# The same program with its SBUF tiles at other addresses: a hybrid decoder layer on one core

## The chip, the core and the metric

The kernel runs on one core of a Trainium2 chip. The metric is the device time of one execution in microseconds (us). The five engines of the core are called PE (TensorE: matrix products; its weight loads are shown apart as PEld), DVE (VectorE), ACT (ScalarE), POOL (GpSimd) and SP (SyncE, which issues DMA transfers). SBUF is the on-chip memory: 128 partitions, in each of which a tile occupies the same byte range. "Address" below means the byte offset in a partition. PSUM is the memory that matrix products are written to.

## What is computed

One decoder layer for 256 tokens of width 2048, in float32. The reference, cut to what matters here:

```python
h = layer_norm(x, ln_in_g, ln_in_b)
parts = split(h @ w_in)                        # LRU group, NSA attention group, memory-attention queries
o_lru = rg_lru_group(...)                      # causal conv, gated linear recurrence, times gelu gate
o_nsa = nsa_group(...)                         # compressed, selected and window attention, 8 heads of 64
o_mem = memory_group(mem_q, mem, w_mem_kv)     # 4 heads of 128 into 256 memory tokens
h = layer_norm(alpha * h + concat(o_lru, o_nsa, o_mem) @ w_out, ln1_g, ln1_b)
up = causal_dwconv(h @ w_up)                   # 2048 -> 2 x 5632
h = layer_norm(alpha * h + (gelu(up_g) * up_u) @ w_down, ln2_g, ln2_b)
```

## The kernel before, in words

All weights are streamed from HBM in chunks of 128 partitions x 1024 float32 (512 KB), in one fixed list of steps (`chunk`, line 93). `run` (171) takes the steps in order; `advance` (143) keeps loads, splits and products apart by a few steps. Every chunk is loaded by SP into one of 4 buffers `raw` (107), rounded by ACT to fp32r into one of 4 buffers `wH` (127), and the rest, raw minus wH, is written by DVE into one of 3 buffers `wL` (135). Activations are held in the same two parts. A product is then three PE products, summed in PSUM: high x high, high x low and low x high.

PE has two operands. The stationary one is a block of 128 x 128 that is loaded into the array (LDWEIGHTS, PEld in the trace); the moving one is streamed through it (MATMUL). Two helpers issue nearly all of them:

- `t_mm` (190, products on lines 194, 195, 197): the weights are stationary and the transposed activations `h` move, 256 columns at a time. 24 products a chunk. It serves the projection w_in (28 column blocks, about 60 to 290 us of the run) and the up projection (88 column blocks, about 390 to 886 us).
- `m_mm` (200, lines 205, 206, 208): the activations are stationary and the weights move, 512 columns at a time. It serves the output projection w_out (activations `oH`, `oL`; about 300 to 390 us), the down projection (`actH`, `actL`; about 886 to 1135 us), half of the memory projection, and the chunks `wvg` with 280 columns.

The first 60 us are the memory projection; its other half is on line 272, where `oH`, `oL`, which hold the split memory tokens there, move by 256 columns past `wH`, `wL`.

In the last column group of w_out, some chunks are split into tiles that are free by then instead of `wH` and `wL`: `lruR`, `lruI`, `lruT`, `qmem`, `kmem`, `vmem`, `qn`, `xc0` (the argument `alt`, 842). In the last column group of the down projection the eight tiles `h0` to `h7` serve so (922).

Tiles get their addresses from pools, in the order in which a pool's tiles are first asked for: first `fix` (60), which lives throughout, then `ws` (61) with raw, wH and wL, then `sm` (62), and last `mx` (65), the tiles of the mixers, whose place is given to the pool `ff` (966) with `actH`, `actL` and four gain and bias tiles after the output projection. Every tile named so far that holds 1024 float32 is 4096 bytes long, so buffers of one name lie at the same place modulo 4096. The order of the work does not depend on the addresses: the schedule is written by hand (66).

Of the kernel before, what the change touches and what calls it, by code (L numbers as in the profile page):

```python
# [21 lines left out]
F32 = mybir.dt.float32  # L22
F32R = mybir.dt.float32r
BF = mybir.dt.bfloat16
# [6 lines left out]
S = 256  # L31
KT = D // 128
# [23 lines left out]
def hymba_layer(ctx, tc, x, memT, params, rows, wab, w1, wmem, win, wvg, wout, wup, wdn, out):  # L56
# [3 lines left out]
    fix = ctx.enter_context(tc.tile_pool(name="fix", bufs=1))  # L60
# [4 lines left out]
    mx = mixstack.enter_context(tc.tile_pool(name="mx", bufs=1))  # L65
    ctx.enter_context(tc.manual_schedule())

    prm = fix.tile([128, NP1], F32, name="prm")
    prm2 = mx.tile([128, NP - NP1], F32, name="prm2")
    hq = [fix.tile([128, 4, S], F32R, name="h%d" % i) for i in range(8)]  # L70

    def hH(kt, cols=slice(0, S)):
# [2 lines left out]
    def hL(kt, cols=slice(0, S)):  # L75
        return hq[4 + kt // 4][:, kt % 4, cols]
    res = fix.tile([128, 2, D], F32, name="res")
    negh = fix.tile([128, 1], F32, name="negh")
    identb = fix.tile([128, 128], BF, name="identb")
    diagb = fix.tile([128, 2, 128], BF, name="diagb")  # L80
    cmaskb = fix.tile([128, 2, 60], BF, name="cmaskb")
    ident = prm[:, _P["ident"]]

    def P(name, i=0, n=1):
# [134 lines left out]
        V.tensor_scalar(dst, src, mv[:, 0:1], rs[:, 1:2], op0=OP.subtract, op1=OP.mult)  # L219


    oH = mx.tile([128, KT, S], F32R, name="oH")
    oL = mx.tile([128, KT, S], F32R, name="oL")
    mraw = {}

    def aH(kt, cols):
# [232 lines left out]
                  done_vg if kts[-1] == KT - 1 else None)  # L459


    kcmp = mx.tile([128, 32], F32, name="kcmp")
    vcmp = mx.tile([128, 2, 64], F32, name="vcmp")
    hidv = mx.tile([64, 2, 4, 32], F32, name="hidv")
    hidk = mx.tile([64, 32], F32, name="hidk")

    def cmp_mm(a):
        def mm(w, _):
# [92 lines left out]
            split_act(oH[:, 12 + h, :], oL[:, 12 + h, :], o[:, :S])  # L561
            yield

    cv = mx.tile([128, 2, 8], F32, name="cv")

    def lru_consts():

        t = mx.tile([128, 6, 8], F32, name="lc")
        lam = P("lam", 0, 8)
        ab, e, z, z2, s, den = (t[:, i, :] for i in range(6))  # L570
        V.tensor_scalar(z, lam, -1.0, None, op0=OP.mult)
        V.tensor_tensor(ab, z, lam, op=OP.max)
        A.activation(e, ab, AF.Exp, scale=-1.0)
        V.tensor_scalar(den, e, 2.0, None, op0=OP.add)
        V.reciprocal(den, den)
        yield
        V.tensor_scalar(ab, z, 0.0, None, op0=OP.max)
        V.tensor_mul(z, e, den)
        V.tensor_mul(z2, z, z)
        V.tensor_scalar(s, z2, 1.0 / 17, 1.0 / 15, op0=OP.mult, op1=OP.add)  # L580
        for k in (13, 11, 9, 7, 5, 3, 1):
            V.tensor_mul(s, s, z2)
            V.tensor_scalar(s, s, 1.0 / k, None, op0=OP.add)
            if k % 4 == 3:
                yield
        V.tensor_mul(s, s, z)
        V.scalar_tensor_tensor(s, s, 2.0, ab, op0=OP.mult, op1=OP.add)
        V.tensor_scalar(cv[:, 0, :], s, -8.0, None, op0=OP.mult)
        V.tensor_scalar(cv[:, 1, :], s, 8.0, None, op0=OP.mult)
        yield  # L590
# [35 lines left out]
            yield  # L626

    pcd = mx.tile([128, 4, 128], F32, name="pcd")
    pc = mx.tile([128, 128], F32, name="pc")
    outs = {}  # L630

    def nsa_gates(q, g):
# [73 lines left out]
        yield  # L706


    st1 = [fix.tile([128, 24], F32, name="st%d" % i) for i in range(2)]
    KORD = [12, 13, 14, 15, 8, 9, 10, 11, 0, 1, 2, 3, 4, 5, 6, 7]  # L710

    def residual(acc, m, nb, st):
# [358 lines left out]
```

## Time and profile before

| | |
|---|---|
| median of 3 runs | 1147.9 us (1147.19 to 1149.84) |
| the profiled execution, its own time | 1146.88 us |
| its span, first to last instruction | 1145.1 us |
| PE busy | 1120.7 us (98%) |
| PE weight loads busy (beside PE) | 1029.3 us (90%) |
| DVE busy | 734.6 us (64%) |
| ACT busy | 565.3 us (49%) |
| DMA, mean over the span | 185 GB/s |

Busy time is the union of an engine's instructions. Products on PE overlap: one is shown as 279 ns long where the next one starts after some 117 ns, so the rate is read from start times and not from the mean of one. A group line gives the line of the kernel, engine, operation, what it writes and reads, shapes, the count, busy time and the mean of one, and behind the last bar the idle time before it.

### The profile page before, as it was taken

Reading aid. Unit: us, or ns where it says so; the run is one execution under the profiler, and the core shown is the slowest. Engines: PE = TensorE matmul, PEld = TensorE weight load, DVE = VectorE, ACT = ScalarE, POOL = GpSimd, SP = SyncE. Lnnn points to the kernel's source line nnn. Section 1 sums busy time; section 2 is a strip of 40 time slices with the busy share of each in tenths; the row PEclk is TensorE's granted clock in tenths of the full one; section 3 lists DMA queues with packets and bytes.
Section 4 is the critical chain, followed back from the end, with each engine's and each line's share of the span. In section 5 each row is a group of like instructions: output and inputs, shape, how many; then the busy total and the mean of one; then the engine's idle time right before and its main releaser. Section 6 shows DMA issues by size and latency. Waiting matters only on the chain. (4 is left out here: it accounts for less than half of the span.)

```text
span 1145.1 us, 19315 instructions
## 1 busy us (share of the span) xinstructions
PE 1120.7 (98%) x7848; PEld 1029.3 (90%) x7848; DVE 734.6 (64%) x1073; ACT 565.3 (49%) x829; POOL 15.3 (1%) x26
## 2 busy tenths in 40 slices
PE   8999999999999899999999999999999999999996
PEld 7889878899988799999999999999999888888884
DVE  6778645567856776666666666666666845454546
ACT  5744444567744555555555555555555433343440
POOL 0200000000000000000000000000000000000000
PEclk9999999999999999999999999999999999999998
DMA  9666322344566466556565656555555776666662
GB/s 339 236 230 218 112 92 93 110 148 151 175 196 181 144 244 197 184 185 188 181 200 176 201 183 198 184 185 186 182 199 179 227 244 197 189 191 193 188 197 93
DMA packets 58984, 211.81 MB, mean 185 GB/s; under 512 B 6544, under 2 KB 6672, under 8 KB 58768
## 3 DMA queue, kind: packets, MB, share of 16 engines
q1 hardware_dynamic: 57024, 203.25, 54.9%
q0 software_dynamic: 1872, 7.34, 1.9%
q8 instruction: 61, 1.00, 0.4%
q14 instruction: 27, 0.22, 0.1%
HBM read 208.47 MB, written 2.10 MB: 184 GB/s over the span
## 5 line engine op out<-in xcount | busy, mean ns | idle before, releaser
L135 DVE TENSOR_TENSOR wL<-raw,wH 128x1024 fp32r<-128x1024 f32 (+2 forms) x367 | 441.5, 1215 | 163.0 <-PE sc L208 118.4
L127 ACT ACTIVATE wH<-raw 128x1024 fp32r<-128x1024 f32 (+2 forms) x367 | 375.6, 1046 | 200.2 <-PE sc L206 163.7
L194 PE MATMUL acc<-h,wH 128*128 128x256 f32 x1152 | 281.1, 284 | 1.4 <-ACT h L187 1.4
L195 PE MATMUL acc<-h,wH 128*128 128x256 f32 x1152 | 276.1, 279 | 0.7 <-DVE h L188 0.7
L194 PEld LDWEIGHTS acc<-h,wH 128*128 128x128 f32 x1152 | 216.7, 188 | 2.1 <-ACT h L187 1.6
L195 PEld LDWEIGHTS acc<-h,wH 128*128 128x128 f32 x1152 | 217.3, 189 | 1.4 <-DVE h L188 1.1
L194 PE MATMUL sc<-h,wH 128*128 128x256 f32 x704 | 168.5, 280 | 0.0
L195 PE MATMUL sc<-h,wH 128*128 128x256 f32 x704 | 168.3, 279 | 0.0
L197 PE MATMUL acc<-h,wL 128*128 128x256 f32 x1152 | 158.8, 279 | 0.0
L197 PEld LDWEIGHTS acc<-h,wL 128*128 128x128 f32 x1152 | 145.3, 188 | 0.0
L195 PEld LDWEIGHTS sc<-h,wH 128*128 128x128 f32 x704 | 132.7, 188 | 0.0
L194 PEld LDWEIGHTS sc<-h,wH 128*128 128x128 f32 x704 | 131.8, 187 | 0.0
L197 PE MATMUL sc<-h,wL 128*128 128x256 f32 x704 | 97.4, 279 | 0.0
L877 DVE SCALAR_TENSOR_TENSOR tn<-sc,prm,tn 128x255 f32<-128x255 f32 x88 | 42.4, 482 | 82.6 <-ACT tn L874 81.0
L197 PEld LDWEIGHTS sc<-h,wL 128*128 128x128 f32 x704 | 89.0, 188 | 0.0
L877 DVE SCALAR_TENSOR_TENSOR tn<-acc,prm,tn 128x255 f32<-128x255 f32 x88 | 42.4, 482 | 44.1 <-ACT tn L874 42.5
L205 PE MATMUL sc<-wH,actH 128*128 128x512 f32 x168 | 66.0, 393 | 0.0
L205 PE MATMUL acc<-wH,actH 128*128 128x512 f32 x168 | 66.0, 393 | 0.0
L206 PE MATMUL acc<-wH,actL 128*128 128x512 f32 x168 | 65.7, 391 | 0.0
L206 PE MATMUL sc<-wH,actL 128*128 128x512 f32 x168 | 65.7, 391 | 0.0
L874 ACT ACTIVATE tn<-sc,prm 128x256 f32<-128x256 f32 x44 | 24.8, 564 | 63.4 <-PE sc L197 63.4
L208 PE MATMUL sc<-wL,actH 128*128 128x512 f32 x168 | 51.9, 390 | 0.0
(294 smaller groups left out, 1213.1 us busy)
## 6 DMA issues: line engine op xcount, KB each, us to landing
raw<-in_wup_dram SPq DMA_DIRECT2D x176, 512.0 KB, 4.3
raw<-in_wdn_dram SPq DMA_DIRECT2D x88, 512.0 KB, 4.3
raw<-in_win_dram SPq DMA_DIRECT2D x56, 512.0 KB, 3.3
raw<-in_wout_dram SPq DMA_DIRECT2D x32, 512.0 KB, 4.2
raw<-in_wmem_dram SPq DMA_DIRECT2D x15, 512.0 KB, 6.9
raw<-in_wvg_dram SPq DMA_DIRECT2D x5, 420.0 KB, 4.1
res<-in_x_dram SPq DMA_DIRECT2D x4, 512.0 KB, 7.6
g<-in_rows_dram POOLq DMA_DIRECT2D x4, 512.0 KB, 6.2
```

What stands on the lines that cost most here:

```text
L127: A.activation(h[:, s], raws[j][:, s], AF.Copy)
L135: V.tensor_sub(l[:, s], r[:, s], splits[j][0][:, s].bitcast(F32))
L194: T.matmul(acc, w, hH(kt), start=(first and a == 0), stop=False, skip_group_check=True)
L195: T.matmul(acc, w, hL(kt), start=False, stop=False, skip_group_check=True)
L197: T.matmul(acc, l[:, a * 128:(a + 1) * 128], hH(kt), start=False, stop=(last and a == n - 1), skip_group_check=True)
L205: T.matmul(acc, xh(kt, ms), h[:, w], start=(first and a == 0), stop=False)
L206: T.matmul(acc, xl(kt, ms), h[:, w], start=False, stop=False)
L208: T.matmul(acc, xh(kt, ms), l[:, a * N:(a + 1) * N], start=False, stop=(last and a == n - 1))
L874: A.activation(t, src, AF.Identity, scale=P("fcw", cb * 3 + 2), bias=P("fcb", cb))
L877: V.scalar_tensor_tensor(t[:, s:], src[:, :S - s], P("fcw", cb * 3 + k), t[:, s:], op0=OP.mult, op1=OP.add)
```

## The change

Tiles are asked for in another order, and a tile of 544 bytes that nobody uses is put in (`gap0`). No instruction is added, removed or moved, on any engine, and no wait: the two programs differ in addresses alone. The whole of it:

```diff
     prm = fix.tile([128, NP1], F32, name="prm")
+    kcmp = mx.tile([128, 32], F32, name="kcmp")
+    vcmp = mx.tile([128, 2, 64], F32, name="vcmp")
+    hidv = mx.tile([64, 2, 4, 32], F32, name="hidv")
+    hidk = mx.tile([64, 32], F32, name="hidk")
+    cv = mx.tile([128, 2, 8], F32, name="cv")
+    pc = mx.tile([128, 128], F32, name="pc")
+    oH = mx.tile([128, KT, S], F32R, name="oH")
+    oL = mx.tile([128, KT, S], F32R, name="oL")
     prm2 = mx.tile([128, NP - NP1], F32, name="prm2")
-    hq = [fix.tile([128, 4, S], F32R, name="h%d" % i) for i in range(8)]
...
-    res = fix.tile([128, 2, D], F32, name="res")
     negh = fix.tile([128, 1], F32, name="negh")
     identb = fix.tile([128, 128], BF, name="identb")
     diagb = fix.tile([128, 2, 128], BF, name="diagb")
     cmaskb = fix.tile([128, 2, 60], BF, name="cmaskb")
+    st1 = [fix.tile([128, 24], F32, name="st%d" % i) for i in range(2)]
+    fix.tile([128, 136], F32, name="gap0")
+    hq = [fix.tile([128, 4, S], F32R, name="h%d" % i) for i in range(8)]
...
+    res = fix.tile([128, 2, D], F32, name="res")
```

(The lines that asked for `oH`, `oL`, `kcmp`, `vcmp`, `hidv`, `hidk`, `cv`, `pc` and `st1` further down are gone.) The addresses in the two built programs, and what is left of them modulo 4096 and 256:

| tiles | address before | mod 4096 (256) | address after | mod 4096 (256) |
|---|---|---|---|---|
| h0 (h1 to h7 follow at 4096 each) | 18688 | 2304 (0) | 20480 | 0 (0) |
| res | 51456 | 2304 (0) | 53248 | 0 (0) |
| raw, 4 buffers | 69088 | 3552 (224) | 69632 | 0 (0) |
| wH, 4 buffers | 85472 | 3552 (224) | 86016 | 0 (0) |
| wL, 3 buffers | 101856 | 3552 (224) | 102400 | 0 (0) |
| oH | 122912 | 32 (32) | 122880 | 0 (0) |
| oL | 139296 | 32 (32) | 139264 | 0 (0) |
| kmem | 155680 | 32 (32) | 158592 | 2944 (128) |
| vmem | 159776 | 32 (32) | 162688 | 2944 (128) |
| lruR | 180832 | 608 (96) | 181376 | 1152 (128) |
| lruI | 185952 | 1632 (96) | 186496 | 2176 (128) |
| xc0 | 190048 | 1632 (96) | 190592 | 2176 (128) |
| lruT | 198240 | 1632 (96) | 198784 | 2176 (128) |
| qn | 212768 | 3872 (32) | 213312 | 320 (64) |
| actH | 119968 | 1184 (160) | 120512 | 1728 (192) |
| actL | 165024 | 1184 (160) | 165568 | 1728 (192) |

Inside a tile every operand of PE starts at a multiple of 512 bytes from the tile's start, but for the 280-column chunks, whose blocks lie 1120 bytes apart.

## Rows read from the trace of the kernel before

**Rows 1.** The page: busy time by engine, then the two costliest groups off PE.

```profile
PE 1120.7 (98%) x7848; PEld 1029.3 (90%) x7848; DVE 734.6 (64%) x1073; ACT 565.3 (49%) x829; POOL 15.3 (1%) x26
...
L135 DVE TENSOR_TENSOR wL<-raw,wH 128x1024 fp32r<-128x1024 f32 (+2 forms) x367 | 441.5, 1215 | 163.0 <-PE sc L208 118.4
L127 ACT ACTIVATE wH<-raw 128x1024 fp32r<-128x1024 f32 (+2 forms) x367 | 375.6, 1046 | 200.2 <-PE sc L206 163.7
```

**Rows 2.** Busy time in four stretches: w_in, up projection, w_out, down projection.

```profile
core 0: us, PE busy (x) PEld busy (x) DVE busy (x) ACT busy (x) POOL busy (x), PEclk, DMA share, GB/s
70.00:290.00 220.00, 218.34 (x1658) 194.40 (x1657) 141.43 (x306) 119.34 (x247) 0.00 (x0) 1.00 0.42 134
400.00:880.00 480.00, 480.00 (x4117) 480.00 (x4116) 320.92 (x438) 250.35 (x350) 2.15 (x4) 1.00 0.59 192
300.00:370.00 70.00, 70.00 (x305) 56.58 (x305) 46.50 (x58) 33.53 (x37) 0.00 (x0) 1.00 0.65 195
890.00:1110.00 220.00, 220.00 (x972) 180.91 (x971) 116.89 (x105) 86.36 (x83) 2.11 (x4) 1.00 0.66 202
```

**Rows 3.** Groups of instructions, shapes kept apart: PE's products, for their counts.

```profile
L194 PE MATMUL acc<-h,wH 128*128 128x256 f32 x1152 | 281.1, 284 | 1.4 <-ACT h L187 1.4
L194 PE MATMUL sc<-h,wH 128*128 128x256 f32 x704 | 168.5, 280 | 0.0
...
L205 PE MATMUL sc<-wH,actH 128*128 128x512 f32 x168 | 66.0, 393 | 0.0
L205 PE MATMUL acc<-wH,actH 128*128 128x512 f32 x168 | 66.0, 393 | 0.0
...
L205 PE MATMUL sc<-wH,oH 128*128 128x512 f32 x56 | 22.0, 393 | 0.0
```

**Rows 4.** Timeline of PE, up projection (columns: start us, length us, what, count).

```profile
600.92 0.28 PE L194 MATMUL acc<-h,wH 128*128 128x256 f32 x1
601.04 0.28 PE L195 MATMUL acc<-h,wH 128*128 128x256 f32 x1
...
606.52 0.28 PE L194 MATMUL sc<-h,wH 128*128 128x256 f32 x1
```

**Rows 5.** Timeline of PE, output projection.

```profile
339.95 0.39 PE L205 MATMUL acc<-wH,oH 128*128 128x512 f32 x1
...
342.75 0.39 PE L205 MATMUL acc<-wH,oH 128*128 128x512 f32 x1
```

**Rows 6.** Timeline of PE, down projection, last column group, where its weights change tiles.

```profile
1117.36 0.39 PE L205 MATMUL acc<-wH,actH 128*128 128x512 f32 x1
...
1120.11 0.39 PE L205 MATMUL acc<-wH,actH 128*128 128x512 f32 x1
...
1122.89 0.40 PE L205 MATMUL acc<-h,actH 128*128 128x512 f32 x1
...
1126.63 0.62 PE L208 MATMUL acc<-h,actH 128*128 128x512 f32 x2
```

**Rows 7.** Timeline of PE, output projection, last column group, first half.

```profile
378.21 0.39 PE L205 MATMUL acc<-lruR,oH 128*128 128x512 f32 x1
...
379.58 0.39 PE L205 MATMUL acc<-lruT,oH 128*128 128x512 f32 x1
...
380.73 0.39 PE L206 MATMUL acc<-kmem,oL 128*128 128x512 f32 x1
...
382.77 0.63 PE L208 MATMUL acc<-xc,oH 128*128 128x512 f32 x2
```

**Rows 8.** Timeline of PE, the same column group's second half, after transposes.

```profile
388.49 0.40 PE L206 MATMUL sc<-kmem,oL 128*128 128x512 f32 x1
...
389.20 0.62 PE L208 MATMUL sc<-vmem,oH 128*128 128x512 f32 x2
```

**Rows 9.** Timeline of PE, memory projection, two chunks of line 272.

```profile
44.25 1.10 PE L272 MATMUL acc<-oL,wH 128*128 128x256 f32 x8
...
46.13 0.40 PE L205 MATMUL acc<-wH,oH 128*128 128x512 f32 x1
...
51.32 1.07 PE L272 MATMUL acc<-oL,wH 128*128 128x256 f32 x8
...
53.14 0.60 PE L340 MATMUL sc<-prm,res 128*128 128x128 f32 x4
```

**Rows 10.** Timeline of PE, the chunks of 280 columns.

```profile
95.21 0.29 PE L205 MATMUL acc<-wH,h 128*128 128x280 f32 x1
...
97.53 0.29 PE L205 MATMUL acc<-wH,h 128*128 128x280 f32 x1
```

More of the change, by code (lines that the diff above doesn't have):

```diff
@@ L68, in hymba_layer @@
     prm = fix.tile([128, NP1], F32, name="prm")
-    prm2 = mx.tile([128, NP - NP1], F32, name="prm2")
+    kcmp = mx.tile([128, 32], F32, name="kcmp")
[6 more added lines that the diff above has]
+    oL = mx.tile([128, KT, S], F32R, name="oL")
+    prm2 = mx.tile([128, NP - NP1], F32, name="prm2")
+    negh = fix.tile([128, 1], F32, name="negh")
+    identb = fix.tile([128, 128], BF, name="identb")
+    diagb = fix.tile([128, 2, 128], BF, name="diagb")
+    cmaskb = fix.tile([128, 2, 60], BF, name="cmaskb")
+    st1 = [fix.tile([128, 24], F32, name="st%d" % i) for i in range(2)]
+    fix.tile([128, 136], F32, name="gap0")
     hq = [fix.tile([128, 4, S], F32R, name="h%d" % i) for i in range(8)]
@@ L77, in hymba_layer @@
     res = fix.tile([128, 2, D], F32, name="res")
[L78 to L81, printed above, removed]
     ident = prm[:, _P["ident"]]
@@ L219, in normalise @@
         V.tensor_scalar(dst, src, mv[:, 0:1], rs[:, 1:2], op0=OP.subtract, op1=OP.mult)
-    oH = mx.tile([128, KT, S], F32R, name="oH")
-    oL = mx.tile([128, KT, S], F32R, name="oL")
     mraw = {}
@@ L459, in vg_chunks @@
                   done_vg if kts[-1] == KT - 1 else None)
[L462 to L465, printed above, removed]
     def cmp_mm(a):
@@ L562, in mem_attention @@
             yield
-    cv = mx.tile([128, 2, 8], F32, name="cv")
     def lru_consts():
@@ L628, in hymba_layer @@
     pcd = mx.tile([128, 4, 128], F32, name="pcd")
-    pc = mx.tile([128, 128], F32, name="pc")
     outs = {}
@@ L706, in nsa_head @@
         yield
-    st1 = [fix.tile([128, 24], F32, name="st%d" % i) for i in range(2)]
     KORD = [12, 13, 14, 15, 8, 9, 10, 11, 0, 1, 2, 3, 4, 5, 6, 7]
```

## The prediction

> **What bounds the kernel now.** I read the page's busy line first: PE is busy for 98% of the span, DVE for 64%, ACT for 49% [rows 1]. Then the busy time by stretch, since the share is a mean over stages [rows 2]: in the up projection, the output projection and the down projection PE is busy for the whole of the stretch, in the w_in projection for 218.34 of 220 us. So the sequence of products sets the time, and nothing waits ahead of it. The granted clock is 1.00 in all four stretches, the upper of its two levels (2.4 GHz), so the clock explains no difference of rate between them. What the change can alter is the time from one product to the next, and that is what the third view, the timeline of PE, is read for.
>
> **Rates before.** I write M for the moving operand's address and W for the stationary one's, both modulo 256, and give every rate per product of 512 columns (a 256-column product counts half). M and W come from the table of addresses, the rates from starts:
> - Up projection, M 0, W 224: 48 products of 256 columns from 600.92 to 606.52, 5.60 us, 116.7 ns each [rows 4]. That is 233.3 per 512.
> - Output projection, M 224, W 32: 12 products in 2.80 us, 233.3 ns [rows 5].
> - Down projection, M 224, W 160: 12 in 2.75 us, 229.2 ns; with the h tiles as weights, M 0 and the same W: 16 in 3.74 us, 233.8 ns [rows 6]. The same stage, the same stationary data, and the rate goes with the moving tile's place.
> - Last group of w_out, W 32 throughout: tiles lruR, lruI, lruT at M 96, 6 in 1.37 us, 228.3 ns; kmem, vmem, qn at M 32, 9 in 2.04 us, 226.7 ns [rows 7].
> - Memory projection, M 32, W 224: one chunk 16 products of 256 columns in 1.88 us, 235 per 512, the other 16 in 1.82 us, 227.5 [rows 9].
> - The 280-column chunks, M 224, 64 and 160 in turn, W 0: 18 in 2.32 us, 128.9 ns, 235.7 per 512 [rows 10].
>
> There is thus a fast rate near 226.7, a slow one near 233.3 that most stretches share, and one between. The extra 6.6 ns per 512 columns is the same share, 2.9%, for 256-column products (116.7 against 113.3), although those load a new stationary block twice as often per column. It does not look like a cost per instruction.
>
> **How I read them.** Ordered by W minus M modulo 256: 0 gives 226.7; 192 gives 228.3, 229.2, and in the memory projection once 227.5 and once 235; 32, 64, 96, 160 and 224 give 233 to 236. My reading is that the two reads of PE, which run side by side (PEld is busy 480.00 of 480 us in the up projection [rows 2]), get into each other's way, and that the distance of their addresses sets how much; distance 0 is best. The case against it is kmem in the second half: distance 0 again, and 3 products in 0.71 us, 236.7 ns, right behind the transposes [rows 8]. I take that for a start that had not settled yet, since the 9 products at distance 0 in the first half followed on others without a break.
>
> **The change part by part.** It moves no instruction and no wait, so the terms are counts times differences of rate.
> - Products with h moving: 1152 + 704 on line 194 [rows 3], as many on 195 and on 197, together 5568. Distance goes from 224 to 0. At 116.7 - 113.3 = 3.4 ns each: 18.9 us off. Of these 88 x 48 = 4224 (14.4 us) lie in the up projection, where PE never idles; 28 x 48 = 1344 (4.6 us) in w_in, where it idles 1.66 us in 220, so I count them whole.
> - Output projection with wH, wL moving: 56 + 56 products on each of three lines [rows 3], 336, distance 64 to 0. At 233.3 - 226.7 = 6.6 ns: 2.2 us off.
> - Down projection: 168 + 168 on each of three lines, 1008 [rows 3]. Distance 192 before (160 - 224) and 192 after (192 - 0): no difference. The 48 products with the h tiles go from distance 160 to 192: 4.6 ns each (233.8 - 229.2), 0.2 us off.
> - The tiles lruR to xc0 in w_out go to distance 128 or 192, which no row shows: at most 48 x 6.6 = 0.3 us on, and I take that.
> - Memory projection and 280-column chunks: 192 products of 256 columns (line 272), 96 of 512 and 96 of 280. The first 60 us wait on loads and splits, and the blocks of 280 keep three different distances: nothing, with 384 x 3.4 = 1.3 us either way as the bound.
> - ACT's and DVE's splits: raw, wH and wL lie at one place modulo 4096 before and after, so their distances to each other stay. Should one of them become 10% longer all the same, DVE's 320.92 us of 480 in the up projection [rows 2] have the room. PE's work covers them, and if that cover were gone each 1% of DVE's 441.5 us [rows 1] would be 4.4 us.
>
> Sum: 18.9 + 2.2 + 0.2 - 0.3 = 21.0 us off. The profiled execution took 1146.88 us for a span of 1145.1, so it would come to 1125.9; the median of the runs stands 1.0 above it, and I predict **1126.9 us**. The bounds of the one large term: the fast rate is seen with 256 columns too [rows 9], so 3.4 ns stands at one end; at the rate between (229 per 512, 114.5 per 256) 2.2 ns are left, 12.2 us instead of 18.9, and if the distance does not matter in this stage it is nothing; a loss is worked out below.
>
> **The rivals.**
> - *No change.* The slow rate would be the moving tile's own: every stretch whose M is 0 is slow (up projection, w_in, the h tiles as weights), and h stays at M 0. Then the 18.9 us do not come; and the down projection, if it keeps its rate by its distance, stays too: 1147.9, or 1145.7 with the output projection's 2.2. Against it: M 224 is slow in w_out and not in the down projection, so M alone does not decide. The Trainium skill (SBUF — State Buffer, "Who interferes with whom") gives PE two independent read ports, one for each operand, and says that PE never waits on anyone; by it no address could matter and the time would be 1147.9 as well. The rows disagree with it so far: 229.2 against 233.8 ns in one stage [rows 6].
> - *Slower.* If it is M 0 that makes a stretch slow, then wH and wL, which go from 224 to 0, take the down projection with them: 1008 products x 4.6 ns = 4.6 us on, place: the 240 us behind 886. The time is 1152.5. It decides as soon as the down projection's products start over 231.5 ns apart (midway) while those of the up projection stay at 116.7. For it: the h tiles as weights, M 0, slow at once [rows 6]. The rate of [rows 10] in place of 233.3 everywhere in the 5568 products would add 5568 x 1.2 = 6.7 us more, 1159; no stretch with aligned tiles alone shows what happens, so I keep that as a tail.
> - *The rate between.* Distance 0 helps, but with 256 columns only to 114.5: 21.0 - 6.7 = 14.3 off, 1133.6.
>
> That the tiles don't lie where the change says is no case: the built program has them there.
>
> **How the numbers follow.** A measurement of this kernel can tell some 0.2%, 2.3 us, from no change. Distance 0 at the full fast rate: 0.35, 1126.9. The rate between: 0.15, 1133.6. No change: 0.25. Slower: 0.25. So faster 0.5, same 0.25, slower 0.25. The forecast's own range with the rate between is 1124 to 1137 (the bound of 1.3 us and the spread of the runs beyond either time). The range that leaves out no more than 2 in 10 has to take in no change and the 1152.5 of the slower case: 1124 to 1153.5.
>
> **What would show it.** Right: 48 products of the up projection in 5.44 us instead of 5.60, w_out at 12 in 2.72, the down projection unchanged at 12 in 2.75, PE still busy throughout, ACT's and DVE's means within 2% of 1046 and 1215 ns. Wrong: an up projection still at 116.7, or a down projection at 233; also idle time on PE behind ACT or DVE, which would mean that the splits became the bound.

## The result, and the profile after

| | before | changed |
|---|---|---|
| median of 4 runs, us | 1148.87 (1147.19 to 1150.99) | 1163.67 (1162.3 to 1164.79) |
| profiled execution: own time, span, us | 1146.88, 1145.1 | 1162.3, 1160.5 |

The change makes the kernel slower: the ratio is 1.0122, with a 95% interval of 1.0098 to 1.0145. The forecast was 1126.9 us, and the time lies above the end of the range, 1153.5.

The page of the changed kernel, first the busy time by engine, then the same two groups as in [rows 1] (their lines are now 146 and 138):

```profile
PE 1136.2 (98%) x7848; PEld 1047.2 (90%) x7848; DVE 734.4 (63%) x1073; ACT 565.6 (49%) x829; POOL 15.3 (1%) x26
...
L146 DVE TENSOR_TENSOR wL<-raw,wH 128x1024 fp32r<-128x1024 f32 (+2 forms) x367 | 441.3, 1215 | 162.4 <-PE sc L219 117.8
L138 ACT ACTIVATE wH<-raw 128x1024 fp32r<-128x1024 f32 (+2 forms) x367 | 375.5, 1045 | 199.4 <-PE sc L217 153.0
```

PE's busy time grew by 15.5 us, from 1120.7 to 1136.2, with the same 7848 instructions; the span grew by 15.4. DVE's splits take 1215 ns as before, ACT's 1045 instead of 1046. So nothing new is waited for: the products themselves take longer.

Busy time by stretch, changed kernel (w_in, up projection, w_out, down projection):

```profile
core 0: us, PE busy (x) PEld busy (x) DVE busy (x) ACT busy (x) POOL busy (x), PEclk, DMA share, GB/s
70.00:290.00 220.00, 218.70 (x1634) 194.71 (x1634) 140.69 (x306) 116.11 (x242) 0.00 (x0) 1.00 0.41 133
400.00:900.00 500.00, 500.00 (x4167) 499.92 (x4166) 324.39 (x445) 254.21 (x359) 2.15 (x4) 1.00 0.57 186
300.00:370.00 70.00, 70.00 (x329) 58.75 (x328) 47.87 (x62) 34.50 (x39) 0.00 (x0) 1.00 0.66 196
910.00:1120.00 210.00, 210.00 (x919) 172.32 (x918) 111.94 (x99) 82.94 (x79) 2.11 (x4) 1.00 0.66 202
```

The up projection now has 4167 products in 500 us, 120.0 ns each; [rows 2] had 4117 in 480, 116.6. The clock is 1.00 in both, the upper level of 2.4 GHz, so it is not the clock. The single products say the same. Timeline of PE, changed kernel: the up projection (48 products from the first row to the second), then w_out and the down projection (12 products each), then the h tiles as weights (16):

```profile
601.42 1.12 PE L208 MATMUL acc<-h,wL 128*128 128x256 f32 x8
...
607.18 1.00 PE L208 MATMUL sc<-h,wL 128*128 128x256 f32 x7
...
339.92 0.39 PE L216 MATMUL acc<-wH,oH 128*128 128x512 f32 x1
...
342.64 0.39 PE L216 MATMUL acc<-wH,oH 128*128 128x512 f32 x1
...
1132.89 0.39 PE L216 MATMUL acc<-wH,actH 128*128 128x512 f32 x1
...
1135.64 0.39 PE L216 MATMUL acc<-wH,actH 128*128 128x512 f32 x1
...
1138.38 0.39 PE L216 MATMUL acc<-h,actH 128*128 128x512 f32 x1
...
1142.04 0.62 PE L219 MATMUL acc<-h,actH 128*128 128x512 f32 x2
```

| products | distance before, after | ns before | ns after | count x difference, us |
|---|---|---|---|---|
| h moving, 256 columns | 224, 0 | 116.7 [rows 4] | 5.76 us / 48 = 120.0 | 5568 x 3.3 = +18.4 |
| w_out, 512 columns | 64, 0 | 233.3 [rows 5] | 2.72 / 12 = 226.7 | 336 x -6.6 = -2.2 |
| down projection, 512 | 192, 192 | 229.2 [rows 6] | 2.75 / 12 = 229.2 | 0 |
| h tiles as weights, 512 | 160, 192 | 233.8 [rows 6] | 3.66 / 16 = 228.8 | 48 x -5.0 = -0.2 |

"Distance" is, as in the prediction, stationary address minus moving address modulo 256. The sum is +16.0 us; the spans differ by 15.4 and the medians by 14.8. All of the loss is in the products with h moving, and the other three terms came as forecast. At one and the same distance, 0, products of 512 columns became quicker and products of 256 columns slower. The memory projection says so on other tiles: there `oH` and `oL` move by 256 columns, and their distance went from 192 to 0. Timeline of PE, changed kernel, 16 products from the first row to the second:

```profile
44.54 1.12 PE L281 MATMUL acc<-oL,wH 128*128 128x256 f32 x8
...
46.46 0.40 PE L216 MATMUL acc<-wH,oH 128*128 128x512 f32 x1
```

1.92 us are 120.0 ns a product; [rows 9] had 117.5 and 113.75.

### The profile page after: what moved, and what is told of

The parts are those of the page before. It is cut to its first block, busy times and chain, and to the rows that moved or that the text cites. A ratio compares the mean times of both kernels' runs of the same rounds, so it can differ in the third digit from the quotient of the medians.

```text
span 1160.5 us, 19315 instructions
## 1 busy us (share of the span) xinstructions
PE 1136.2 (98%) x7848; PEld 1047.2 (90%) x7848; DVE 734.4 (63%) x1073; ACT 565.6 (49%) x829; POOL 15.3 (1%) x26
## 5 line engine op out<-in xcount | busy, mean ns | idle before, releaser
L146 DVE TENSOR_TENSOR wL<-raw,wH 128x1024 fp32r<-128x1024 f32 (+2 forms) x367 | 441.3, 1215 | 162.4 <-PE sc L219 117.8
L138 ACT ACTIVATE wH<-raw 128x1024 fp32r<-128x1024 f32 (+2 forms) x367 | 375.5, 1045 | 199.4 <-PE sc L217 153.0
L205 PE MATMUL acc<-h,wH 128*128 128x256 f32 x1152 | 287.3, 287 | 1.5 <-ACT h L198 1.5
L206 PE MATMUL acc<-h,wH 128*128 128x256 f32 x1152 | 282.9, 283 | 0.6 <-DVE h L199 0.6
L205 PEld LDWEIGHTS acc<-h,wH 128*128 128x128 f32 x1152 | 220.7, 192 | 2.2 <-ACT h L198 1.7
L206 PEld LDWEIGHTS acc<-h,wH 128*128 128x128 f32 x1152 | 220.7, 192 | 1.4 <-DVE h L199 1.0
L205 PE MATMUL sc<-h,wH 128*128 128x256 f32 x704 | 173.0, 283 | 0.0
L206 PE MATMUL sc<-h,wH 128*128 128x256 f32 x704 | 173.0, 283 | 0.0
L208 PE MATMUL acc<-h,wL 128*128 128x256 f32 x1152 | 162.6, 283 | 0.0
L208 PEld LDWEIGHTS acc<-h,wL 128*128 128x128 f32 x1152 | 149.0, 192 | 0.0
L206 PEld LDWEIGHTS sc<-h,wH 128*128 128x128 f32 x704 | 135.2, 192 | 0.0
L205 PEld LDWEIGHTS sc<-h,wH 128*128 128x128 f32 x704 | 135.2, 192 | 0.0
L208 PE MATMUL sc<-h,wL 128*128 128x256 f32 x704 | 99.8, 283 | 0.0
L875 ACT ACTIVATE tn<-acc,prm 128x256 f32<-128x256 f32 x44 | 24.9, 566 | 58.0 <-PE acc L208 58.0
```

The costliest lines, as they stand in the source:

```text
L138: A.activation(h[:, s], raws[j][:, s], AF.Copy)
L146: V.tensor_sub(l[:, s], r[:, s], splits[j][0][:, s].bitcast(F32))
L205: T.matmul(acc, w, hH(kt), start=(first and a == 0), stop=False, skip_group_check=True)
L206: T.matmul(acc, w, hL(kt), start=False, stop=False, skip_group_check=True)
L208: T.matmul(acc, l[:, a * 128:(a + 1) * 128], hH(kt), start=False, stop=(last and a == n - 1), skip_group_check=True)
L875: A.activation(t, src, AF.Identity, scale=P("fcw", cb * 3 + 2), bias=P("fcb", cb))
```

## Experiments

**Theory A** after the result: the rate hangs on the distance, but a product of 256 columns has another function of it than one of 512, and 0 is a bad place for it. **Rival B**: the alignment of h and the weights itself (multiples of 64 or of 4096 bytes) is slow. **Rival C**: it is the place of h modulo a larger power of two.

Most kernels below move h alone. The small tiles go behind `res`, a gap of g bytes lies ahead of h and one of 544 - g behind `res`, so that weight buffers and mixers' outputs stay at multiples of 4096. The edit for g = 32, against the changed kernel (the others differ in the two numbers of the gaps):

```diff
-    negh = fix.tile([128, 1], F32, name="negh")
...
-    st1 = [fix.tile([128, 24], F32, name="st%d" % i) for i in range(2)]
-    fix.tile([128, 136], F32, name="gap0")
+    fix.tile([128, 8], F32, name="gap0")
     hq = [fix.tile([128, 4, S], F32R, name="h%d" % i) for i in range(8)]
...
     res = fix.tile([128, 2, D], F32, name="res")
+    negh = fix.tile([128, 1], F32, name="negh")
...
+    st1 = [fix.tile([128, 24], F32, name="st%d" % i) for i in range(2)]
+    fix.tile([128, 128], F32, name="gap1")
```

### Is it the alignment, or the distance?

The first kernel leaves h's distance at 0 and takes all alignment away, by moving everything behind the gap by 32 bytes:

```diff
-    fix.tile([128, 136], F32, name="gap0")
+    fix.tile([128, 144], F32, name="gap0")
```

> The changed kernel with an unused tile 32 bytes longer: h, res, raw, wH, wL, oH, oL, actH and actL all lie 32 bytes higher, so no start is a multiple of 64 any more and every distance W - M is that of the changed kernel. If the distance alone decides: up projection 120.0 ns per 256-column product, output projection 226.7 per 512, down projection 229.2, time within 3 us of 1163.7. If alignment to 64 bytes or more is what makes the 256-column products slow: up projection back at 116.7 or below, some 18 us faster, near 1145.

The second has g = 0 (h and `res` back at their old place): h's distance is 1792 modulo 4096, still 0 modulo 256.

> The weights, oH and oL stay at multiples of 4096, h and res go back to where they were (18688, 2304 modulo 4096): distance 0 modulo 256 as in the changed kernel, 1792 modulo 4096, 256 modulo 512. If the distance modulo 256 decides: 120.0 ns in the up projection and 1163.7 us. If what hurts is that both operands start at the same place modulo 512, or modulo 4096: 116.7 or less, at or below 1146.

The third has g = 32, which gives h back the distance 224 that it had before the change, with everything else as in the changed kernel.

> As the run with h at its old place, but h and res 32 bytes higher: distance 224 modulo 256, that of the kernel before, while the weights stay aligned. If the distance decides: 116.7 ns in the up projection again; the output projection keeps its new 226.7, so the time is 1148.9 - 2.2 = about 1146. If h's or the weights' own alignment decides: 120.0 stays, 1163.

They took 1164.71, 1164.7 and 1148.49 us; the kernel before took 1150.46 beside them. Timeline of PE in the up projection, 48 products from the first row to the second, for the first kernel (h and all that lies behind it moved by 32 bytes):

```profile
600.95 1.12 PE L208 MATMUL acc<-h,wL 128*128 128x256 f32 x8
...
606.71 1.12 PE L208 MATMUL sc<-h,wL 128*128 128x256 f32 x8
```

for the second (h at its old place):

```profile
600.94 1.12 PE L208 MATMUL acc<-h,wL 128*128 128x256 f32 x8
...
606.70 1.12 PE L208 MATMUL sc<-h,wL 128*128 128x256 f32 x8
```

and for the third (h 32 bytes above that):

```profile
601.59 1.10 PE L209 MATMUL sc<-h,wL 128*128 128x256 f32 x8
...
607.19 1.10 PE L209 MATMUL acc<-h,wL 128*128 128x256 f32 x8
```

5.76 us is 120.0 ns a product, 5.60 is 116.7. With neither h nor a weight buffer at a multiple of 64 the products are as slow as in the changed kernel, and with the weights still aligned, but h 32 bytes further, they are as quick as before. Rival B falls. The second kernel has 120.0 ns too, so a shift of h by 1792 bytes with the same remainder modulo 256 changes nothing: rival C falls for this pair, and nothing in it needs a period longer than 256. The third kernel's gain on before, 2.0 us in one execution of each, fits w_out's 2.2.

### The function of the distance

g = 64, 96, 128, 160, 192 and 224:

> As before, h and res 64 bytes higher: distance 192 modulo 256, at which the memory projection of the kernel before (line 272, 256 columns) ran one chunk at 113.6 and the others at 117.5 ns. If the distance decides and the faster of the two is where it settles: 113.4 ns, 5568 x 6.6 = 37 us below the changed kernel, about 1127. If the slower: 117.5, about 1150. If alignment to 64 bytes decides: 120.0 and 1163.

> h and res 96 bytes above their old place, weights aligned: distance 160 modulo 256. In the kernel before, 512-column products ran at 233.8 at this distance. If the distance sets one rate per distance whatever the width: 116.9 ns in the up projection, about 1148. If, as at distance 0, the 256-column products have a scale of their own: another value; up to 120.0 and 1165.

> Distance 128 modulo 256, which nothing has shown yet. If nearness of the two reads is what hurts 256-column products (0 slowest), the farthest distance is the best: 113.3 ns everywhere, w_in included, and about 1129. If the pattern repeats every 128 bytes: 120.0 and 1165.

> Distance 96 modulo 256. By nearness: between distance 64 and 128, 113.3 to 116.7 ns, 1129 to 1148. By a pattern of 128 bytes, as distance 224: 116.7 ns and about 1148.

> Distance 64 modulo 256, at which the output projection of the kernel before ran at 233.3 per 512. If only the size of the distance counts and not its sign, as distance 192: 113.4 in the up projection, 117.6 in w_in, about 1136. If the sign counts: 116.7 or more, 1148 to 1165.

> Distance 32 modulo 256, the last of the eight. Between 0 (120.0) and 64 (113.4): if the cost falls off with the distance, some 117; by the mirror of distance 224, 116.7 and about 1148.

| distance of the h products | ns, 256 columns (up projection) | one execution, us (before beside it) | ns, 512 columns |
|---|---|---|---|
| 0 | 120.0 | 1164.7 (1150.46) | 226.7 to 228 |
| 32 | 118.3 | 1156.19 (1149.96) | 232.6 |
| 64 | 113.3 here; 117.7 in other executions | 1131.79 (1150.7) | 233 |
| 96 | 118.7 | 1157.82 (1150.7) | 235 |
| 128 | 118.7 | 1158.2 (1150.7) | 232 |
| 160 | 120.0 | 1165.36 (1150.7) | 234 |
| 192 | 113.3 here; 117.7 in other executions | 1135.63 (1150.46) | 229 to 230 |
| 224 | 116.7 | 1148.49 (1150.46) | 232 to 234 |

The last column comes from w_out and from the h tiles as weights, whose distance moves with h (192 - g, and 224 again in the last experiment below), each over 16 products or more. Neither nearness of the two addresses nor a pattern of 128 bytes, the orders that the expectations had, describes the 256-column rates: 128 has 118.7, and 32 and 96 are slower than 224. The distances 64 and 192 are alike; 32 and 224, or 96 and 160, are not. Two rows of the timeline of PE, up projection, 48 products apart, for g = 192 (distance 64):

```profile
601.52 1.07 PE L209 MATMUL sc<-h,wL 128*128 128x256 f32 x8
...
606.97 1.07 PE L209 MATMUL acc<-h,wL 128*128 128x256 f32 x8
```

and for g = 96 (distance 160):

```profile
601.48 1.12 PE L209 MATMUL acc<-h,wL 128*128 128x256 f32 x8
...
607.24 1.12 PE L209 MATMUL sc<-h,wL 128*128 128x256 f32 x8
```

5.45 us against 5.76: one tile group moved by 96 bytes makes 6.5 ns a product. Distance 0, best for 512 columns, is (with 160) worst for 256, and 64, where 512 columns are near their worst, has 256 columns' best rate. The times follow from the counts: for distance 160, 5568 x 3.3 - 2.2 = +16.2 us, and 14.7 were measured. For g = 64 (distance 192), 4224 x -3.4 in the up projection, 1344 x +0.9 in w_in (117.6 in the mean) and -2.2 make -15.4, and -14.8 were measured. That +0.9 is the first sign of something else: with the same addresses w_in ran at another rate than the up projection. Timeline of PE, g = 64, w_in, 48 products in 5.66 us, 117.9 ns:

```profile
292.32 1.10 PE L209 MATMUL acc<-h,wL 128*128 128x256 f32 x8
...
297.98 1.10 PE L209 MATMUL acc<-h,wL 128*128 128x256 f32 x8
```

One rival is left open by the addresses: `raw`, `wH` and `wL` share one remainder in every kernel here, so h's distance from what ACT, DVE and the loads touch moves along with its distance from the stationary blocks. The trace of the changed kernel answers it. Two stretches of the up projection (columns as above), one with DVE and ACT idle while loads arrive, one with both busy and hardly a load:

```profile
814.30:815.50 1.20, 1.20 (x12) 1.20 (x11) 0.00 (x0) 0.00 (x0) 0.00 (x0) 1.00 0.81 328
818.30:819.50 1.20, 1.20 (x13) 1.20 (x12) 1.20 (x2) 1.20 (x2) 0.00 (x0) 1.00 0.04 14
```

Timeline of PE there, 8 products from the first row to the second and 16 from the third to the fourth:

```profile
814.54 1.12 PE L208 MATMUL sc<-h,wL 128*128 128x256 f32 x8
815.50 0.28 PE L205 MATMUL acc<-h,wH 128*128 128x256 f32 x1
...
818.38 0.28 PE L205 MATMUL acc<-h,wH 128*128 128x256 f32 x1
...
820.30 0.40 PE L208 MATMUL acc<-h,wL 128*128 128x256 f32 x2
```

0.96 us and 1.92 us are both 120.0 ns a product. The cost of distance 0 is there whether or not another engine or a load is at work.

### Is the width what sets the function?

The changed kernel, with each 512-column product of `m_mm` issued as two of 256 columns, each with its own load of the stationary block (the third product, with the low part, is halved the same way and cut here):

```diff
+        W = 256 if N == 512 else N
+        cuts = [slice(c, c + W) for c in range(0, N, W)]
+
+        def mm(stat, src, a, start, stop):
+            for c, cut in enumerate(cuts):
+                T.matmul(acc[:, cut], stat, src[:, a * N + cut.start:a * N + cut.stop], start=(start and c == 0),
+                         stop=stop, skip_group_check=True)
...
-            T.matmul(acc, xh(kt, ms), h[:, w], start=(first and a == 0), stop=False)
-            T.matmul(acc, xl(kt, ms), h[:, w], start=False, stop=False)
+            mm(xh(kt, ms), h, a, first and a == 0, False)
+            mm(xl(kt, ms), h, a, False, False)
```

> The changed kernel with every 512-column product of the helper m_mm issued as two of 256 columns, each with its own load of the same stationary block; addresses unchanged. If the width of the product (how often a stationary block is loaded) is what turns distance 0 from best to worst: output projection 240 per 512 columns instead of 226.7; the down projection (distance 192) 226.8 or 235.2, the two states seen at 192 with 256 columns. If what differs is that h moves and weights stand still: output projection near 227 still, down projection 229.2. The time goes up by some 4 us in the first case (336 x 13.3 = 4.5), with up to 1008 x 6 = 6 us more from the down projection.

It took 1167.8 us, 3.1 more than the two kernels at distance 0 above. Timeline of PE, this kernel: w_out (distance 0), 12 products from the first row to the second, then the down projection (distance 192), 12 as well:

```profile
341.11 0.40 PE L219 MATMUL acc<-wH,oH 128*128 128x256 f32 x2
...
342.55 0.40 PE L219 MATMUL sc<-wH,oH 128*128 128x256 f32 x2
...
1000.85 0.39 PE L219 MATMUL sc<-wH,actH 128*128 128x256 f32 x2
...
1002.21 0.39 PE L219 MATMUL acc<-wH,actH 128*128 128x256 f32 x2
```

In w_out 1.44 us / 12 = 120.0 ns, 240 for 512 columns instead of 226.7: same tiles, same distance, and only the width (and with it the number of stationary loads) is another. In the down projection 113.3 ns, 226.7 for 512 columns instead of 229.2. So theory A holds, both ways, for the product's form. By these rates it is 336 x 13.3 - 1008 x 2.5 = 2.0 us on. The run does not part the width from the stationary load that each half has of its own.

### Without any alignment

The kernel before, with 96 bytes behind its small tiles and no other edit. h stays where it was (M 0), the weight buffers and the mixers' outputs move from 224 and 32 to 64 and 128, so the h products get distance 64, w_out keeps its 64, and no weight buffer or output lies at a multiple of 4096:

```diff
+    fix.tile([128, 24], F32, name="gap0")
```

> The kernel before with one line more: an unused tile of 96 bytes behind the fixed tiles, so that h stays and everything behind it moves by 96. Nothing lies at a multiple of 4096 (wH 3648, oH 128, h 2304 modulo 4096). Distance of the h products 64 instead of 224, all other distances of 512-column products as before. If the distance modulo 256 decides: up projection 113.4 ns, w_out still 233.3, down projection still 229.2, 5568 x 3.3 = 18.4 us less than the kernel before, ratio 0.984. If alignment has a part in it: less than half of that.

Three of four executions took 1132.2, 1132.77 and 1133.54 us, the fourth 1156.27; the ratio of the three to before (1149.96) is 0.9852, interval 0.9838 to 0.9866. This time the stationary side was moved and h was not, and the rate is the one that h's own move to distance 64 gave: 113.3 ns in the up projection, while w_out stays at 233.3. By the terms it would be 5568 x -3.4 = -18.9 us; 0.0148 x 1149.96 = 17.0 were measured. In w_in the trace has 114.6 ns in the mean and not 113.3, which is 1344 x 1.3 = 1.7 us of the difference. The fourth execution was not traced.

### The best version, and two rates at one distance

The last two terms with it: h at distance 64 (g = 192), and 64 bytes ahead of `actH`, which bring the down projection to distance 0.

```diff
+    ff.tile([128, 16], F32, name="gap2")
```

> h and res 192 bytes above their old place (distance 64, as in the run that took 1131.8), weights, oH and oL at multiples of 4096 (distance 0), and 64 bytes of gap in front of actH, so that actH and actL come to distance 0 too. By the distance: up projection 113.4, w_out 226.7, down projection 226.7 instead of 229.2, 1008 x 2.5 = 2.5 us below 1131.8, so 1129.3, ratio to before 0.982. If the down projection has a scale of its own it stays at 229.2 or rises.

> The same kernel as e10. If the rate is drawn by execution: two groups again, near 1129 and 1148, in about equal shares, and none above the kernel before. If it depends on the chip: one group.

It is one kernel, measured twice. Of its 14 executions 7 took 1127.7 to 1130.1 us and 7 took 1146.7 to 1149.5; before took 1149.96 (median of 11) beside the first and 1150.0 (median of 17) beside the second. The quicker executions have a ratio of 0.9824 (0.981 to 0.9838) to before in the first measurement and 0.9812 (0.9789 to 0.9835) in the second. The profiled execution of the first took 1149.49 us, that of the second 1128.87, so the traces show what differs. Timeline of PE, up projection, 48 products apart, first the one of 1149.49:

```profile
602.02 1.11 PE L209 MATMUL sc<-h,wL 128*128 128x256 f32 x8
...
607.67 1.11 PE L209 MATMUL acc<-h,wL 128*128 128x256 f32 x8
```

then the one of 1128.87:

```profile
600.68 1.07 PE L209 MATMUL sc<-h,wL 128*128 128x256 f32 x8
...
606.12 1.07 PE L209 MATMUL acc<-h,wL 128*128 128x256 f32 x8
```

5.65 us is 117.7 ns a product, 5.44 is 113.3. The program and the addresses are the same, and each rate is kept through the up projection. By the first products of each stage in the two timelines, w_out begins at 301.88 and 301.21 us, the up projection at 397.78 and 397.02, the down projection at 896.93 and 876.30. So of the 20.6 us between the two, 0.7 come from ahead of w_out and 19.9 from the up projection, where 4224 x 4.4 = 18.6. The down projection is at 226.7 ns in both.

In w_in both executions have both rates. Timeline of PE, w_in of the execution of 1149.49, two chunks with products of other lines between them, 15 products from the first row of each pair to the second:

```profile
171.54 0.28 PE L207 MATMUL acc<-h,wH 128*128 128x256 f32 x1
...
173.31 1.10 PE L209 MATMUL acc<-h,wL 128*128 128x256 f32 x8
...
177.57 0.28 PE L207 MATMUL acc<-h,wH 128*128 128x256 f32 x1
...
179.27 1.07 PE L209 MATMUL acc<-h,wL 128*128 128x256 f32 x8
```

1.77 us is 118.0 ns, 1.70 is 113.3. In the four traces at distance 64, 11 to 13 of w_in's 37 unbroken sequences of 24 products or more (behind 75 us) settle at the slower rate and the others at the quicker; in the two traces at 192 all 37 are slow, while the up projection is quick in one (g = 64) and slow in the other. In all six a sequence settles within its first ten products and then keeps its rate to its end. The up projection is one unbroken sequence of some 4200 products, so one settling decides 18.6 us; that accounts for the two groups of times.

Three kernels asked what chooses the rate. All have `actH` at distance 0; they differ in where the eight tiles of h lie: all at 192; the four of the high part at 64 and the four of the low part at 192; and the reverse. The edit of the second, cut to the tiles of h:

```diff
+    hq = {}
+    for i, before in ((0, 192), (1, 0), (2, 0), (3, 0), (4, 128), (5, 0), (6, 0), (7, 0)):
+        if before:
+            fix.tile([128, before // 4], F32, name="gap%d" % i)
+        hq[i] = fix.tile([128, 4, S], F32R, name="h%d" % i)
```

> As the version with distance 64 and the down projection at distance 0, but h at distance 192. If both distances have the two rates alike: some executions near 1130, some near 1149. If distance 192 always ends in the fast rate in the up projection, as in its one run so far, and in 117.6 in w_in: all executions near 1133.

> High part of h at distance 64, low part at 192; all else as e13. If a rate is kept from product to product, lines 194 and 195 now alternate between two distances and 197 repeats one: one state is left, either 113.3 (all executions near 1129) or about 117.7 (all near 1148). If it is drawn anew by execution: two times again.

> The reverse: high part of h at distance 192, low part at 64. Same expectations: one time for all executions (1129 or 1148) if the state is kept from product to product, two if it is drawn by execution.

At 192, 11 of 12 executions took 1149.88 to 1152.45 us and one 1132.74. High part at 64, low at 192: nine of ten 1149.43 to 1151.48, one 1142.07, ratio 0.9998 (0.9982 to 1.0014). The reverse: ten within 1147.88 to 1149.46, ratio 0.9985 (0.9974 to 0.9995). The fourth kernel changes the distance by chunk instead, tiles 0, 1, 4 and 5 at 64 and the others at 192:

> The first half of the contraction (h0, h1 and their low parts) at distance 64, the second at 192, so the distance changes with each chunk of 24 products. If the switch draws the state anew: the rate varies from chunk to chunk about (113.3 + 117.7) / 2 = 115.5, and executions agree near 1139. If the state passes over the switch: two times, near 1130 and 1149.

Its ten executions fall into two groups, 1138.94 to 1141.77 (five) and 1148.17 to 1149.47 (five), ratio 0.9948 (0.9925 to 0.9972). The quicker group is near 1139, as expected for half of the products at the quick rate, and the slower at 1149; neither expectation had the two together. The trace is of a slow one, with 117.8 ns in the up projection. Alternating distances does not force the quick rate. The share of quick executions differs with the placement, and what chooses between them stays open. The clock at the start of the up projection does not choose it: it begins at a granted clock of 0.50 with g = 64 and g = 192, which went on at 113.3 ns, and in the execution of 1149.49, which went on at 117.7.

A version without that choice: the best version with h back at distance 224 (g = 32), where the other traces (the kernel before, g = 32) show one rate, 116.7 ns.

> h at distance 224 as in the kernel before, oH, oL, actH and actL at distance 0 to the weights. By the distance: 116.7 in the up projection, w_out 226.7 instead of 233.3 (336 x 6.6 = 2.2 us), down projection 226.7 instead of 229.2 (1008 x 2.5 = 2.5 us): 4.7 us less than the kernel before, ratio 0.996, and all executions within 2 us of each other.

Of twelve executions eleven took 1144.72 to 1146.22 us and one 1149.79; ratio 0.9959 (0.9947 to 0.9972). By the terms it is 2.2 us for w_out and 1008 x 2.5 = 2.5 for the down projection, 4.7 in all, and 0.0041 x 1150 is 4.7.

So two versions beat the kernel before: this one by 0.4%, and the best version, which was under the median of before in all 14 of its executions and 1.8% under it in half.

## Why the prediction was wrong

- **The step that failed** is the first term, "At 116.7 - 113.3 = 3.4 ns each: 18.9 us off". The count was right (5568) and the place too (PE's sequence alone sets the end); the price was not. The fast rate at distance 0 had been read from products of 512 columns [rows 7] and carried over to 256 by the remark that the extra share is the same 2.9%. At distance 0 a 256-column product takes 120.0 ns: 18.4 us on. The experiment with halved products shows that this is a matter of the product's form (width, or loads per column), on the same tiles.
- The bound that should have caught it, "the fast rate is seen with 256 columns too [rows 9]", rested on the memory projection, whose distance is 192 and not 0. No row of before had 256 columns at distance 0; by the bounds the term should have been open on the side of a loss too. And [rows 9] held the second finding: 117.5 and 113.75 ns at one distance, in two chunks of one line, match the two rates of 192 that the experiments show (117.7 and 113.3).
- **Right, but for the two rates at 64 and 192**: that the distance of the two operands and not the place of one sets the rate. h alone, the weights without h, and all together were moved, and the rate went with the difference. The picture behind it, two reads that get into each other's way, was not tested. The Trainium skill (SBUF — State Buffer, "Who interferes with whom"), by which PE waits on no one, would have no address matter; the rows show 113.3 to 120.0 ns for one instruction at one granted clock, 1.00, and the measurement decides.
- **Right**: w_out -2.2 us at 226.7 ns, the down projection unchanged at 229.2, the h tiles as weights -0.2, the splits unchanged, PE busy throughout. The 0.3 us for the tiles lruR to xc0 was a bound; they run at 231.9 ns in the mean, 2.6 more than before, on 48 products 0.1 us.
- **The rivals.** The slower one named another mechanism, the down projection taken along by its moving tiles at 0. That did not happen: its rate stayed, and the loss lies in the up projection and w_in. "No change" by the moving tile's own place is excluded by g = 32 to 224, where M alone moved and the rate went from 113.3 to 120.0 ns. "The rate between" expected 114.5 at distance 0, which no trace has. Nearest to what happened was the tail of 1159: the right 5568 products and the right sign, but priced at 1.2 ns from the 280-column rows [rows 10] where 3.3 were measured, and left outside the range.
- A range for a term whose case no row shows has to be worked out from all rows of the same form: 256-column rows lay between 113.75 and 117.5 over two distances. Their spread, upward as well as downward, times 5568 would have been about 20 us on either side, and 1163.67 inside it.

## What to carry to other kernels

Where PE is busy all the time, read the time from one product to the next in each stage and compare it between stages with their operands' addresses: here a gap of 96 bytes was worth 1.5% in three executions of four, and alignment to 4096 bytes by itself nothing. Carry no rate from one product width to another, and try the placement for the form that holds most of the time. Repeat the executions and trace several of them before believing a gain, since one placement can have two rates, and a long unbroken sequence of products settles on one of them once.

## What the runs showed of the hardware that was not expected

- The rate of an fp32r product at the full granted clock varies with stationary minus moving address modulo 256: 113.3 to 120.0 ns for 256 columns, 226.7 to 235 for 512, in another order. Only multiples of 32 bytes were tried. The cause inside the engine is not shown: a conflict of the two reads was the prediction's picture, and no run tests it. What is shown is that the cost does not need DVE, ACT or a load at work.
- At the lower clock the placement costs nothing. At the start of the up projection, and in w_in, some traces have a granted clock of 0.50 (1.2 GHz) for a few us, and there, behind the first ones, the h products start 213 to 214 ns apart at all eight distances. The kernel with g = 0 (distance 0, 120.0 ns at the upper clock), where PE had waited 3.80 us for DVE ahead of 398.75 us; a stretch in the columns as above:

```profile
402.00:403.90 1.90, 1.90 (x10) 1.90 (x10) 1.22 (x4) 1.65 (x5) 0.00 (x0) 0.50 0.00 0
```

Timeline of PE there, 9 products from the first row to the second:

```profile
401.98 0.41 PE L206 MATMUL acc<-h,wH 128*128 128x256 f32 x1
...
403.90 0.41 PE L208 MATMUL acc<-h,wL 128*128 128x256 f32 x1
```

1.92 us is 213.3 ns. Half of it, 106.7, is an estimate of what a product would take at the upper clock if nothing were lost; no trace shows a stretch at it, and by it even the best placement, 113.3, is 6% above.

- At distances 64 and 192 the 256-column products have two rates, 113.3 and 117.7 ns, kept over thousands of products. In the kernel before with 96 bytes more, the up projection begins at about 118 ns and turns. Timeline of PE, that kernel:

```profile
398.85 0.40 PE L198 MATMUL acc<-h,wL 128*128 128x256 f32 x2
...
399.56 0.40 PE L198 MATMUL acc<-h,wL 128*128 128x256 f32 x2
399.80 0.38 PE L341 MATMUL o<-prm,res 128*128 128x128 f32 x2
...
400.13 0.28 PE L196 MATMUL acc<-h,wH 128*128 128x256 f32 x1
...
400.72 0.28 PE L195 MATMUL acc<-h,wH 128*128 128x256 f32 x1
...
401.11 0.28 PE L195 MATMUL acc<-h,wH 128*128 128x256 f32 x1
...
402.03 0.39 PE L198 MATMUL sc<-h,wL 128*128 128x256 f32 x2
...
404.75 0.39 PE L198 MATMUL acc<-h,wL 128*128 128x256 f32 x2
```

From 398.85 to 399.56 there are 6 products in 0.71 us, 118 ns. Two products of another kind (line 341) break the sequence, and the rate is not changed by them: from 400.13 to 400.72 there are 5 products in 0.59 us, 118 ns again. Then two products take 0.39 us, a pause of some 0.15 us, and behind it the rate turns: from 402.03 to 404.75 there are 24 in 2.72, 113.3, and that rate stays. So the rate changes behind a break of the sequence, but not behind every one, and at distance 192 none of w_in's breaks behind 75 us changed it. What in a break chooses the rate is not shown: no run added or removed one.
